# Weight sums and gate rows kept in DRAM in another layout, fetched in larger pieces, with VectorE's gating placed later in its order

## The chip, the core and the metric

The kernel runs on one core of one Trainium2 chip. The metric is the device time of one execution in microseconds (us). Each engine of the core (TensorE, here PE; VectorE, DVE; ScalarE, ACT; GpSimd, POOL; and the queue of SyncE, SP, which only issues transfers) works through its own list of instructions in program order and waits at semaphores for the others. PEld is TensorE's loading of weights.

## What is computed

One layer of a diffusion trunk on 1024 latent tokens (rows 0 to 7 of 128 tokens) and 128 context tokens (row 8). Both go through an input projection, a position-mixing group A and an attention group B; what concerns this change is the end of the attention and the output projection:

```python
def _back(x, gate, a_out, attn, g_b, w_o):
    y = jnp.concatenate([a_out, attn * jax.nn.silu(g_b)], axis=-1) @ w_o
    return x + gate * y
...
    y_sample = _rmsnorm(xs, final_g)
```

`gate` is a row of 1024 numbers for the latent tokens, another for the context tokens. `w_o` is 1024 x 1024.

## The kernel before

**Split operands.** Matmuls are done in three passes on a high and a low part of each operand (`hi`, `lo`), both stored as float32r. The high part is a rounded copy, the low part is what `lo_of` (L112, on VectorE) subtracts out.

**The output projection by Strassen-Winograd.** The product (latent rows) x `w_o` is done in 2 x 2 blocks with seven products for each pair of rows instead of eight. Four of the seven use a sum of blocks of `w_o` on the right: T1, T2, T3, T4. These *weight sums* depend on `w_o` alone. They are made during the attention in eight units (`t_unit`: subtractions on GpSimd, high part on ScalarE, low part on VectorE) and stored by SP in a DRAM tensor, `tdram` (L253): sum m, quarter k of the contraction, partition, part (high or low), 512 columns. Later they are fetched on GpSimd's DMA queue by `t_piece` (512 KB, both parts of one k) and `t_fetch` (256 KB, one part).

**Order during attention.** One head's scores are shifted by their maximum (`softmax`: L1481 and L1484 find the two maxima, then `nb` is made either by one instruction, L1489, or by a reduction and a product, L1486 and L1487), exponentiated on ScalarE (L1495) and scaled on GpSimd (L1501). Lists of spare work, `his` and `los`, are emptied a few jobs at a time after each head (`spare_hi`, `spare_lo`): splitting `w_o` (GpSimd, then VectorE), splitting row 8 and the first blocks, and the four sums of the first pair of rows (`s_sums`, L806 and L809 on GpSimd). T2 is fetched by a timed job, T3 by four jobs in `his`.

**The final stage.** `final` begins when the attention's tiles are given up (`c_at` is closed) and its tiles (`ep` pool) take their place. Here a small planner (`Plan`) sets the order: every step names its engine, a modelled cost and what it needs; a step is put out as soon as its engine is free and its needs are met in the model. Each engine then runs that order. Fetches are steps on a modelled engine D, one after the other: `gate0` (the latent gate row, read 128 times from `gdram`, 2 KB apart in four rows of 512), T1 and T4 in eight pieces on GpSimd's queue, `own1` (context gate and row 8 of x), rows of x, `fg`.

**Products and their banks.** The products of the final stage run in this order: three that were begun in the attention's last part (A11, A12 and S4 of pair 0, in PSUM banks f0, f1, f2), then S2, S3, S1 of pair 0 (trace names S2_0, S3_0, S1_0), A11 and A12 of pair 1, A22 of pair 0, and so on to pair 3. A product is 12 matmuls of 128 x 512 (L1923 to L1925). Its left operand lies in a ring of three slots (flat area, ringB, ringC), filled by ScalarE (L2149 copies the block to PSUM, L2151 makes the high part) and VectorE (L112, the low part; steps `lo3`, `lo4`, `lo5` for S2_0, S3_0, S1_0). The five PSUM banks are handed on: a product can start in a bank when the step that empties it is done. Bank f1 is emptied by step `m11` of pair 0 (L2197 on VectorE), which multiplies A12 by the gate row; S1_0 takes f1 next.

Of the kernel before, what the change touches and what calls it, by code (L numbers as in the profile page):

```python
# [18 lines left out]
P = 128  # L19
# [75 lines left out]
def tile_hymba_step(ctx: ExitStack, tc: tile.TileContext, I, O):  # L95
# [928 lines left out]
    def gate_steps(j):  # L1024
# [446 lines left out]
    def softmax(t, h, lat_, con_):  # L1471
# [11 lines left out]
        def shift():  # L1483
            V.tensor_reduce(m[:, 1:2], con_, axis=AX.X, op=ALU.max)  # L1484
            if units or his:
                V.tensor_reduce(nb, m, axis=AX.X, op=ALU.max)  # L1486
                V.tensor_scalar(nb, nb, nscl[:, t : t + 1], None, op0=ALU.mult)  # L1487
            else:
                V.scalar_tensor_tensor(nb, m[:, 0:1], m[:, 1:2], nscl[:, t : t + 1], op0=ALU.max, op1=ALU.mult)  # L1489
            later(0.6, exps)  # L1490
            later(1.3, lambda: spare_lo(1))
# [6 lines left out]
        def divide():  # L1498
# [3 lines left out]
            made.add(("e", t, h))  # L1502
            spare_hi(2)
            spare_lo(2)
# [107 lines left out]
    flat = []  # L1612
    for g in range(3):
        cols = area[g].rearrange("p a c -> p (a c)")
        flat.append([cols[:, n * 1024 : (n + 1) * 1024] for n in range(6)])


    his, los, rank = [], [], {}

# [168 lines left out]
    with tc.manual_schedule(engines=engines):  # L1788
# [52 lines left out]
        def first_jobs():  # L1841
# [31 lines left out]
        def t_unit(u, part, more):  # L1873
# [4 lines left out]
            def store(i, part_, src):  # L1878
                for m, j in ((1, 0), (3, 1), (4, 2), (2, 3))[2 * i : 2 * i + 2]:
                    nc.sync.dma_start(f32(tdram[m - 1, k][:, part_, 256 * c : 256 * c + 256]), src[:, j % 2, :])  # L1880

# [29 lines left out]

        def t_fetch(m, k, hi, lo):
            th[m, k], tl[m, k] = hi, lo
            for i, part in enumerate((hi, lo)):
                G.dma_start(part, tdram[m - 1, k][:, i, :])

        def t_piece(m, k, piece):
            th[m, k], tl[m, k] = piece[:, 0:512], piece[:, 512:1024]
            G.dma_start(piece, tdram[m - 1, k].rearrange("p s c -> p (s c)"))

# [105 lines left out]
    tpiece += [kv.tile([P, 1024], F32R, tag=n, name=f"{n}t") for n in ("vh", "vl")]  # L2026
    fg = ep.tile([P, 1024], F32, tag="fg", name="fg")
# [17 lines left out]

    def fetch(key, fn, deps=()):
        last_ = [fetched[0]] if fetched[0] else []
        step(key, "D", 1.35, fn, [*deps, *last_], 0, lag=1.8)
        fetched[0] = "|" + key

    def load_gate():
        gate[0] = ep.tile([P, 1024], F32, name="gate0", tag="gate0")
        nc.sync.dma_start(
            gate[0].rearrange("p (j r) -> p j r", j=4), gdram.rearrange("j (c r) -> c j r", c=2)[0:1].broadcast_to([P, 4, 256])
        )

    own = {}

    def load_own(i, dma):
        t_ = own[i] = ep.tile([P, 1024], F32, tag="xr", name=f"own{i}", bufs=4)  # L2060
        rows = gdram.rearrange("j (c r) -> c j r", c=2)[1:2, 2 * i : 2 * i + 2]
        dma(t_[:, 0:512].rearrange("p (j r) -> p j r", j=2), rows.broadcast_to([P, 2, 256]))
# [93 lines left out]
    for m in range(4):  # L2156
        plan.made[f"s{m}0"] = 0.0
        plan.made[f"T2{m}"] = plan.made[f"T3{m}"] = 0.0

# [17 lines left out]
    def pair(n):  # L2177
# [24 lines left out]
        if True:  # L2202
# [36 lines left out]
            for t in PAIRS[nx]:  # L2239
                fetch(f"x{t}", lambda t=t: load_xr(t), {2: [], 3: ["a81"]}.get(t, [f"y{t - 4}"]))  # L2240

    def products():
        for q in range(1, 28):
            n, name, m = queue[q]
            if q < 3:
                continue
            deps = [f"lo{q}", *([f"{m}{k}" for k in range(4)] if m[0] == "T" else [])]

# [166 lines left out]
```

## Time and profile before

| what | value |
|---|---|
| median of 3 runs | 626.22 us (624.83 to 626.61) |
| the profiled execution | 625.82 us |
| its span, first to last instruction | 624.0 us |
| time around the span | 1.82 us |
| VectorE, ScalarE, GpSimd busy | 428.7, 329.7, 207.8 us |
| bytes moved by DMA | 67.33 MB, mean 108 GB/s |

The profile lists, for one profiled execution, what each engine did at which time, what it waited for, and what the DMA queues moved. In the lists of instructions by time a row has the start in us, the length in us, engine, line, operation, output<-input, shapes and count, and in brackets the idle time of that engine just ahead of it with what ended it. In the tables by window a row has a stretch, its length, the busy time and number of instructions of PE, PEld, DVE, ACT and POOL, TensorE's granted clock as a share of full speed, the mean busy share of the 16 DMA engines, and GB/s. Queue q0 carries what GpSimd issues, q1 what SP issues, q10 what ScalarE issues; a queue's row has packets, MB and the share of the 16 engines' time.

### The profile page before, as it was taken

How to read it: one execution, taken by the hardware profiler on the slowest of the kernel's cores; microseconds unless marked ns; L12 is line 12 of the kernel's file. 1: busy time of each engine (PE TensorE's matmuls, PEld its weight loads, DVE VectorE, ACT ScalarE, POOL GpSimd, SP SyncE). 2: the span in 40 equal slices, each digit the busy share in tenths (PEclk: the TensorE clock that was granted, in tenths of full speed). 3: DMA queues.
4: the chain of work that ended last, by engine and by line, in shares of the span. 5: the costliest groups of instructions: out<-in, count | busy, mean ns of one | idle time of the engine just before them, and what ended most of it. 6: DMA issues, size and time to landing. Idle time of an engine off the chain costs nothing.

```text
span 624.0 us, 10238 instructions
## 1 busy us (share of the span) xinstructions
PE 599.9 (96%) x3671; PEld 540.1 (87%) x3671; DVE 428.7 (69%) x936; ACT 329.7 (53%) x765; POOL 207.8 (33%) x254
## 2 busy tenths in 40 slices
PE   7999999999999999999999999999999999599994
PEld 7578889999989999999988898998999888488884
DVE  3774458897755567566778677767778755268995
ACT  6556754336423345455676556665655543257543
POOL 2461111000000000333363354535434575059741
PEclk9999999999999999999999999999999999799998
DMA  8992010101262033000020143334410058850453
GB/s 309 367 392 86 1 34 2 35 1 46 100 232 84 14 119 125 20 1 1 2 74 1 35 136 126 125 126 133 135 69 35 1 185 241 282 170 8 161 154 151
DMA packets 32083, 67.33 MB, mean 108 GB/s; under 512 B 3472, under 2 KB 18592, under 8 KB 31520
## 3 DMA queue, kind: packets, MB, share of 16 engines
q1 hardware_dynamic: 27872, 55.41, 25.7%
q0 software_dynamic: 2880, 8.39, 4.2%
q10 hardware_dynamic: 1280, 2.88, 1.4%
q8 instruction: 29, 0.48, 0.3%
q14 instruction: 22, 0.18, 0.1%
HBM read 53.45 MB, written 13.21 MB: 107 GB/s over the span
## 4 chain that ended last, share of the span: by engine, by line
PE 76%; DVE 11%; DMA 5%; ACT 4%; issue 2%; SPq 0%; ACTq 0%; DVEq 0%
PE p L954 10%; PE tp L752 8%; PE tp L976 5%; DVE pl L112 4%; PE pT L1562 3%; DVE m L1481 2%; PE zacc L1390 2%; PE zacc L1391 2%; PE zacc L1389 2%; ACT e L1495 2%; PE S L1925 2%; PE S L1923 2%; PE S L1924 2%; DMA gate<-gdram 2%; DMA ada<-in_ada_ss 2%
## 5 line engine op out<-in xcount | busy, mean ns | idle before, releaser
L1501 POOL TENSOR_SCALAR e<-e,rs 128x1280 f32<-128x1280 f32 x32 | 47.0, 1467 | 100.6 <-ACT ph L1566 66.7
L112 DVE TENSOR_TENSOR pl<-pT,ph 128x512 fp32r<-128x512 f32 x81 | 55.4, 687 | 35.6 <-ACT ph L1566 33.8
L1495 ACT ACTIVATE e<-s,nb,scl 128x256 f32<-128x256 f32 x64 | 56.1, 880 | 43.3 <-DVE nb L1487 28.6
L1566 ACT CAST ph<-pT 128x512 fp32r<-128x512 f32 x80 | 46.3, 587 | 33.5 <-PE pT L1562 31.8
L1237 POOL TENSOR_TENSOR kr<-z,rope 128x64 f32<-128x64 f32 x8 | 2.6, 324 | 172.3 <-ACT z L1246 172.3
L752 PE MATMUL tp<-area,w 128*128 128x384 f32 x288 | 52.7, 339 | 0.0
L1562 PE MATMUL pT<-ident,e 128*128 128x128 f32 x320 | 48.4, 274 | 3.4 <-DVE pl L112 2.8
L752 PEld LDWEIGHTS tp<-area,w 128*128 128x128 f32 x288 | 50.6, 188 | 0.4
L1586 PE MATMUL o<-ph,vh 128*128 128x256 f32 x160 | 47.7, 298 | 0.0
L1588 PE MATMUL o<-ph,vl 128*128 128x256 f32 x160 | 45.0, 281 | 0.0
L1587 PE MATMUL o<-pl,vh 128*128 128x256 f32 x160 | 44.9, 281 | 0.0
L1562 PEld LDWEIGHTS pT<-ident,e 128*128 128x128 f32 x320 | 37.0, 140 | 8.4 <-PE at L1605 3.1
L1481 DVE TENSOR_REDUCE m<-s 128x1 f32<-128x1024 f32 x32 | 38.9, 1215 | 1.6 <-PE s L1519 1.6
L1515 PE MATMUL s<-kch,area 128*128 128x512 f32 (+2 forms) x100 | 39.1, 391 | 0.0
L1516 PE MATMUL s<-kcl,area 128*128 128x512 f32 (+2 forms) x100 | 35.3, 353 | 0.0
L1518 PE MATMUL s<-krh,area 128*128 128x512 f32 (+2 forms) x100 | 35.3, 353 | 0.0
L1517 PE MATMUL s<-kch,area 128*128 128x512 f32 (+2 forms) x100 | 35.1, 351 | 0.0
L1519 PE MATMUL s<-krl,area 128*128 128x512 f32 (+2 forms) x100 | 35.1, 351 | 0.0
L976 PE MATMUL tp<-area,w 128*128 128x384 f32 x192 | 35.0, 337 | 0.0
L976 PEld LDWEIGHTS tp<-area,w 128*128 128x128 f32 x192 | 33.6, 188 | 0.4 <-issue 0.4
L1587 PEld LDWEIGHTS o<-pl,vh 128*128 128x128 f32 x160 | 30.2, 189 | 1.3
L1586 PEld LDWEIGHTS o<-ph,vh 128*128 128x128 f32 x160 | 30.1, 188 | 1.4
(666 smaller groups left out, 1725.9 us busy)
## 6 DMA issues: line engine op xcount, KB each, us to landing
ada<-in_ada_ss SPq DMA_DIRECT2D x16, 512.0 KB, 8.5
w2r<-in_w_t SPq DMA_DIRECT2D x12, 512.0 KB, 4.3
x<-in_x SPq DMA_DIRECT2D x9, 512.0 KB, 7.6
adag<-in_ada_g SPq DMA_DIRECT2D x4, 1024.0 KB, 5.0
traw<-in_w_o SPq DMA_DIRECT2D x16, 256.0 KB, 3.5
tdram<-thi SPq DMA_DIRECT2D x32, 128.0 KB, 1.9
tdram<-traw SPq DMA_DIRECT2D x32, 128.0 KB, 1.8
wor<-in_w_o SPq DMA_DIRECT2D x8, 512.0 KB, 3.8
```

The lines of the kernel that those rows point to most:

```text
L112: V.tensor_tensor(lo, src, f32(hi), op=ALU.subtract)
L752: T.matmul(tps[i, g][:, :GW], w_[i][:, k, :], x_[k, g], start=k == 0 and j == 0, stop=k == NK - 1 and j == 2)
L954: T.matmul(banks[key], a_, b_, start=k == 0 and m == 0, stop=k == 3 and m == len(passes) - 1)
L976: T.matmul(tps[c, 2][:, :GW], w_[c][:, k, :], x_[k, 2], start=k == 0 and m == 0, stop=k == NK - 1 and m == 2)
L1481: V.tensor_reduce(m[:, 0:1], lat_, axis=AX.X, op=ALU.max)
L1495: S.activation(e[:, sl], src, AF.Exp, bias=nb, scale=scl[:, t : t + 1], accum_out=su[:, i : i + 1])
L1501: G.tensor_scalar(e, e, rs, 0.0, op0=ALU.mult, op1=ALU.add)
L1562: T.transpose(ps[:, w : w + P], es[t, h][:, c * P : (c + 1) * P], ident)
L1566: later(0.5, lambda: S.copy(ph[:, :w], ps[:, :w]))
L1586: T.matmul(o, vh[:, kt, :], ph[:, sl], start=c == 0, stop=False)
L1587: T.matmul(o, vh[:, kt, :], pl[:, sl], start=False, stop=False)
L1588: T.matmul(o, vl[:, kt, :], ph[:, sl], start=False, stop=c == n - 1)
```

## The change

The gate rows lie in DRAM as two rows of 1024 (latent, context), so that the fetch of `gate0` reads one run of 4 KB for each partition instead of four of 1 KB, and `own` one of 2 KB instead of two of 1 KB. `tdram` is laid out with a partition's four k side by side (16 KB from one partition to the next, 4 KB before), and `t_pieces` fetches two k in one issue of 1 MB: T2 and T1 by two issues each (8 KB runs for each partition), T3 by two (read in 8 KB runs, put in four runs of 2 KB), T4 by one of 1 MB and two of 512 KB. The one-instruction form of `nb` is used for every head without weight-sum units except the last. The list `heavy` holds the sums of pair 0, and one of them, not two, is done after a head while one is next. In the planner the gate counts as landed 4.5 us after its issue instead of 1.8, and T1 and T4 have costs by their sizes.

```diff
-    gdram = gd.tile([4, 512], F32, tag="gdram", name="gdram")
-    tdram = gd.tile([4, 4, P, 2, 512], F32R, tag="tdram", name="tdram")
+    gdram = gd.tile([2, 1024], F32, tag="gdram", name="gdram")
+    tdram = gd.tile([4, P, 4, 2, 512], F32R, tag="tdram", name="tdram")
...
-            nc.sync.dma_start(gdram[j : j + 1, :].rearrange("a (c r) -> (a c) r", c=2), cell["row"])
+            nc.sync.dma_start(gdram[:, 256 * j : 256 * j + 256], cell["row"])
...
-            if units or his:
+            if units or (t, h) == (NS - 1, 3):
...
-            spare_hi(2)
+            spare_hi(1 if his and his[0] in heavy else 2)
...
+                heavy.add(his[-1])
...
-        def t_fetch(m, k, hi, lo):
-            th[m, k], tl[m, k] = hi, lo
-            for i, part in enumerate((hi, lo)):
-                G.dma_start(part, tdram[m - 1, k][:, i, :])
-
-        def t_piece(m, k, piece):
-            th[m, k], tl[m, k] = piece[:, 0:512], piece[:, 512:1024]
-            G.dma_start(piece, tdram[m - 1, k].rearrange("p s c -> p (s c)"))
+        def t_pieces(m, k, hold, wide=512):
+
+            rows = hold.rearrange("p (a c) -> p a c", c=wide)[:, :, wide - 512 :]
+            n = rows.shape[1] // 2
+            for i in range(n):
+                th[m, k + i], tl[m, k + i] = rows[:, 2 * i], rows[:, 2 * i + 1]
+            G.dma_start(rows, tdram[m - 1, :, k : k + n].rearrange("p k s c -> p (k s) c"))
...
-                his.extend([lambda n=n: t_fetch(3, n, woh[n][:, 512:1024], wol[n][:, 512:1024]) for n in range(4)])
+                his.extend([lambda n=n: t_pieces(3, 2 * n, whole[n][:, 0:4096], 1024) for n in range(2)])
...
-        later(2.0, lambda: [t_piece(2, n, flat[2][2 + n]) for n in range(4)])
+        later(2.0, lambda: [t_pieces(2, 2 * n, whole[2][:, 2048 * n + 2048 : 2048 * n + 4096]) for n in range(2)])
...
-    tpiece = [ep.tile([P, 1024], F32R, tag=f"t{i}", name=f"tp{i}") for i in range(6)]
+    t1 = ep.tile([P, 4096], F32R, tag="t1", name="t1")
+    t4 = [ep.tile([P, 2048], F32R, tag="t4", name="t4"), *(kv.tile([P, 1024], F32R, tag=n, name=f"{n}t") for n in ("vh", "vl"))]
...
-    fetch("gate0", load_gate)
-    for m, n in ((1, 0), (4, 4)):
-        for k in range(4):
-            fetch(f"T{m}{k}", lambda m=m, k=k, n=n: t_piece(m, k, tpiece[n + k]))
+    fetch("gate0", load_gate, lag=4.5)
+    for k in (0, 2):
+        fetch(f"T1{k}", lambda k=k: t_pieces(1, k, t1[:, 1024 * k : 1024 * k + 2048]), cost=2.7)
+    for k, piece in ((0, t4[0]), (2, t4[1]), (3, t4[2])):
+        fetch(f"T4{k}", lambda k=k, piece=piece: t_pieces(4, k, piece), cost=1.35 if k else 2.7)
```

On VectorE, at the start of the final stage, before the change (mixB<-f1,gate0 is `m11`; the rows with raw3, raw4, raw5 are `lo3`, `lo4`, `lo5`):

```order
L806 TENSOR_TENSOR f1_5795<-f1_5795,mixA_95 128x512
L112 TENSOR_TENSOR area0_118<-raw3_6088,area0_118 128x512
L2197 TENSOR_TENSOR mixB_2045<-f1_5795,gate0_6074 128x4x128
L112 TENSOR_TENSOR ringB_5593<-raw4_6095,ringB_5593 128x512
L112 TENSOR_TENSOR ringC_5819<-raw5_6112,ringC_5819 128x512
L806 TENSOR_TENSOR mixA_95<-S2_0_6098,mixA_95 128x4x128
L112 TENSOR_TENSOR area0_118<-raw6_6133,area0_118 128x512
```

And with the change:

```order
L806 TENSOR_TENSOR f1_5790<-f1_5790,mixA_95 128x512
L112 TENSOR_TENSOR area0_118<-raw3_6072,area0_118 128x512
L112 TENSOR_TENSOR ringB_5590<-raw4_6078,ringB_5590 128x512
L112 TENSOR_TENSOR ringC_5828<-raw5_6094,ringC_5828 128x512
L2194 TENSOR_TENSOR mixB_2045<-f1_5790,gate0_6058 128x4x128
L806 TENSOR_TENSOR mixA_95<-S2_0_6080,mixA_95 128x4x128
L112 TENSOR_TENSOR area0_118<-raw6_6115,area0_118 128x512
```

`m11` stood ahead of `lo4` and `lo5` and stands behind them now; nothing else moved there. TensorE's order is the same. But S1_0 follows `m11` in bank f1, so its first matmul now waits for `m11`; before, `m11` was done whenever `lo4` was.

On GpSimd, from the scaling of head (7, 1) (e71) to the fetch of T1, before:

```order
L809 TENSOR_TENSOR mixB_2045<-mixA_95 128x4x128
L1501 TENSOR_SCALAR e72_5668<-e72_5668,rs72_5667 128x1280
L809 TENSOR_TENSOR mixA_95<-mixA_95 128x4x128
L809 TENSOR_TENSOR mixB_2045<-mixB_2045 128x4x128
L1501 TENSOR_SCALAR e73_5737<-e73_5737,rs73_5736 128x1280
L115 TENSOR_SCALAR ringC_5819<-mixB_2045 128x512
L1919 DMA area2_120<-tdram_92 128x1024
```

And with the change (area2<-tdram is the fetch of T2):

```order
L1501 TENSOR_SCALAR e72_5664<-e72_5664,rs72_5663 128x1280
L809 TENSOR_TENSOR mixB_2045<-mixA_95 128x4x128
L1501 TENSOR_SCALAR e73_5731<-e73_5731,rs73_5730 128x1280
L809 TENSOR_TENSOR mixA_95<-mixA_95 128x4x128
L809 TENSOR_TENSOR mixB_2045<-mixB_2045 128x4x128
L1919 DMA area2_120<-tdram_92 128x2048
L1919 DMA area2_120<-tdram_92 128x2048
L115 TENSOR_SCALAR ringC_5828<-mixB_2045 128x512
```

Each of the last three sums moved behind the scaling of the next head, and T2 is fetched ahead of the copy to ringC. Further on, all of T3 (three of eight pieces went ahead of it before) is fetched behind the split of the last quarter of `w_o` (wor7).

More of the change, by code (lines that the diff above doesn't have):

```diff
@@ L1612, in tile_hymba_step @@
     flat = []
-    for g in range(3):
-        cols = area[g].rearrange("p a c -> p (a c)")
+    whole = [area[g].rearrange("p a c -> p (a c)") for g in range(3)]
+    for cols in whole:
         flat.append([cols[:, n * 1024 : (n + 1) * 1024] for n in range(6)])
-    his, los, rank = [], [], {}
+    his, los, rank, heavy = [], [], {}, set()
     def split_job(hi, lo, key):
@@ L1879, in store @@
                 for m, j in ((1, 0), (3, 1), (4, 2), (2, 3))[2 * i : 2 * i + 2]:
-                    nc.sync.dma_start(f32(tdram[m - 1, k][:, part_, 256 * c : 256 * c + 256]), src[:, j % 2, :])
+                    nc.sync.dma_start(f32(tdram[m - 1, :, k, part_, 256 * c : 256 * c + 256]), src[:, j % 2, :])
             def high(i):
@@ L2044, in tile_hymba_step, with fetch @@
     fetched = [None]
-    def fetch(key, fn, deps=()):
+    def fetch(key, fn, deps=(), cost=1.35, lag=1.8):
         last_ = [fetched[0]] if fetched[0] else []
-        step(key, "D", 1.35, fn, [*deps, *last_], 0, lag=1.8)
+        step(key, "D", cost, fn, [*deps, *last_], 0, lag=lag)
         fetched[0] = "|" + key
@@ L2052, in load_gate @@
         gate[0] = ep.tile([P, 1024], F32, name="gate0", tag="gate0")
-        nc.sync.dma_start(
-            gate[0].rearrange("p (j r) -> p j r", j=4), gdram.rearrange("j (c r) -> c j r", c=2)[0:1].broadcast_to([P, 4, 256])
-        )
+        nc.sync.dma_start(gate[0], gdram[0:1, :].broadcast_to([P, 1024]))
     own = {}
@@ L2060, in load_own @@
         t_ = own[i] = ep.tile([P, 1024], F32, tag="xr", name=f"own{i}", bufs=4)
[L2061 to L2062 removed]
+        dma(t_[:, 0:512], gdram[1:2, 512 * i : 512 * i + 512].broadcast_to([P, 512]))
         dma(t_[:, 512:1024], I["x"][8][:, 512 * i : 512 * i + 512])
[L2065 to L2068 removed]
+    fetch("gate0", load_gate, lag=4.5)
[3 more added lines that the diff above has]
+        fetch(f"T4{k}", lambda k=k, piece=piece: t_pieces(4, k, piece), cost=1.35 if k else 2.7)
     fetch("own1", lambda: load_own(1, nc.scalar.dma_start))
@@ L2157, in tile_hymba_step @@
         plan.made[f"s{m}0"] = 0.0
-        plan.made[f"T2{m}"] = plan.made[f"T3{m}"] = 0.0
     turn = [None]
@@ L2240, in pair @@
                 fetch(f"x{t}", lambda t=t: load_xr(t), {2: [], 3: ["a81"]}.get(t, [f"y{t - 4}"]))
+    landed = dict(T1=("T10", "T12"), T4=("T40", "T42", "T43"))
     def products():
@@ L2246, in products @@
                 continue
-            deps = [f"lo{q}", *([f"{m}{k}" for k in range(4)] if m[0] == "T" else [])]
+            deps = [f"lo{q}", *landed.get(m, ())]
             def whole(q=q, n=n, name=name):
```

1 line of the change is left out of this document (removed).

## The prediction

> **What bounds the kernel now.** I read the busy table first, then the slices, the chain of waits, and last the rows by time where the chain leaves TensorE. The page's busy row of TensorE, its row of slices, and its row of the granted clock (40 slices of 15.6 us):
>
> ```profile
> PE 599.9 (96%) x3671; PEld 540.1 (87%) x3671; DVE 428.7 (69%) x936; ACT 329.7 (53%) x765; POOL 207.8 (33%) x254
> PE   7999999999999999999999999999999999599994
> PEclk9999999999999999999999999999999999799998
> ```
>
> TensorE is the bound: slices of 9 from the second to the last but one, with one hole, the 35th slice (530 to 546 us), where the clock falls too. The chain of waits names a transfer there, and the table by window shows the stage:
>
> ```profile
> 528.55 11.91 DMA gate<-gdram
> 541.90 0.80 PE S L1925
> 450.00:508.00 58.00, 56.68 (x393) 51.58 (x392) 44.42 (x94) 31.12 (x66) 28.89 (x29) 1.00 0.16 55
> 531.00:547.00 16.00, 9.02 (x31) 6.93 (x30) 3.76 (x7) 3.64 (x7) 1.29 (x1) 0.79 0.74 264
> 547.00:613.00 66.00, 66.00 (x302) 54.52 (x301) 55.27 (x92) 37.61 (x88) 42.38 (x32) 1.00 0.39 128
> ```
>
> From 547 to 613 TensorE never stops, so a product that starts earlier at 546 should carry the end with it. From 531 to 547 it works 9.02 of 16 us. VectorE's rows there, then TensorE's:
>
> ```profile
> 531.00 0.68 DVE L112 TENSOR_TENSOR area<-raw,area 128x512 fp32r<-128x512 f32 x1
> 540.55 0.69 DVE L2197 TENSOR_TENSOR mixB<-f,gate 128x512 f32<-128x512 f32 x1 [8.87 <-DMA gate<-gdram]
> 541.16 0.68 DVE L112 TENSOR_TENSOR ringB<-raw,ringB 128x512 fp32r<-128x512 f32 x1
> 531.58 0.39 PE L1923 MATMUL S<-area,area 128*128 128x512 f32 x1
> 534.30 0.39 PE L1923 MATMUL S<-area,ringB 128*128 128x512 f32 x1
> 534.53 0.39 PE L1924 MATMUL S<-area,ringB 128*128 128x512 f32 x1
> 541.90 0.80 PE L1925 MATMUL S<-area,ringB 128*128 128x512 f32 x1 [6.98 <-DVE ringB L112]
> 546.30 0.40 PE L1923 MATMUL S<-tp,ringC 128*128 128x512 f32 x1
> ```
>
> VectorE stands at `m11` until the gate row lands, and behind it stands `lo4`, for which S3_0's third matmul waits. The 512 KB gate fetch took 12.0 us, since T1 and T4, 4 MB, moved beside it.
>
> **Term 1: the hole.** One product takes 534.30 - 531.58 = 2.72 us. Unhindered, S3_0 would end and S1_0 begin at 534.30 + 2.72 = 537.02; it began at 546.30. The hole is 9.28 us: some 7.1 us of idling, and 2.1 us because the ten matmuls behind it took 4.40 us instead of 2.27. The clock explains that:
>
> ```profile
> 539.00:540.00 1.00, 0.00 (x0) 0.00 (x0) 0.00 (x0) 0.00 (x0) 0.00 (x0) 0.71 1.14 416
> 540.00:541.00 1.00, 0.00 (x0) 0.00 (x0) 0.45 (x1) 0.00 (x0) 0.00 (x0) 0.50 1.06 401
> 546.00:547.00 1.00, 1.00 (x5) 0.81 (x4) 0.00 (x0) 0.80 (x2) 0.00 (x0) 0.87 0.00 0
> ```
>
> In the new order `lo4` and `lo5` need only ScalarE's copies, which are there in time:
>
> ```profile
> 532.12 1.10 ACT L2149 COPY raw<-mixA 128x512 f32<-128x512 f32 x2
> ```
>
> Both end by 533.2, so VectorE ends `lo4` and `lo5` by about 534.6; S3_0's third matmul is due at 534.76. The hole goes at that place: **-9.28 us**.
>
> **Term 2: the last head's shift.** L1489 is long where GpSimd works beside it:
>
> ```profile
> 502.40 1.29 POOL L809 TENSOR_TENSOR mixB<-mixB 128x512 f32<-128x512 f32 x1
> 502.81 0.89 DVE L1489 SCALAR_TENSOR_TENSOR nb<-m,nscl 128x1 f32<-128x1 f32 x1
> 506.89 0.66 PE L1562 MATMUL pT<-ident,e 128*128 128x128 f32 x4 [0.72 <-DVE pl L112]
> L1486 DVE TENSOR_REDUCE nb<-m x20: 154/154/156, 348.9 to 496.9; 128x1 f32<-128x2 f32 x20
> L1487 DVE TENSOR_SCALAR nb<-nb,nscl x20: 212/214/216, 349.1 to 497.1; 128x1 f32<-128x1 f32 x20
> L1489 DVE SCALAR_TENSOR_TENSOR nb<-m,nscl x12: 219/254/1160, 318.1 to 502.8; 128x1 f32<-128x1 f32 x12
> ```
>
> It ended at 503.70 with GpSimd's subtraction (503.69). The two-step form takes 0.40 us here with its gap, so the exponentials, the transposes and TensorE, which idled 0.72 us for them, come **0.49 us** sooner; everything below moves with that. The other five heads go the other way, to L1489: 0.15 us less each where GpSimd is quiet, up to 0.8 us more where it is not (1160 against 370 ns), so +4 us at worst. I take 0: TensorE works 56.68 of 58 us in that stage, so little can be gained, and by the rows of before GpSimd's job ends before or at most 0.4 us behind those five places, as here (the shift comes at 484.39):
>
> ```profile
> 484.06 0.62 POOL L115 TENSOR_SCALAR area<-mixB 128x512 fp32r<-128x512 f32 x1
> ```
>
> **Term 3: the new wait.** S1_0 now waits for `m11`, so for the gate. How the gate shared the queues, in the stretches 532 to 533 and 534 to 535; then the issue of `own` and its queue, almost alone, from 550 to 551 and 551 to 552; last T3's and T1's queue from 526 to 527:
>
> ```profile
> q1 hardware_dynamic: 12, 0.01, 4.5%
> q0 software_dynamic: 78, 0.29, 78.3%
> q1 hardware_dynamic: 85, 0.09, 31.4%
> 549.14 0.40 ACTq L2062 DMA_DIRECT2D own<-gdram  x1
> q10 hardware_dynamic: 126, 0.13, 41.0%
> q10 hardware_dynamic: 144, 0.16, 103.6%
> q0 software_dynamic: 156, 0.29, 106.7%
> ```
>
> Its first packets moved some 4.2 us after the issue at 528.55, behind what q0 had in hand; then they went one to one with T's packets (85 beside 78), 512 of 1 KB in some 6.3 us; `m11` began 1.25 us after the last. Now there are 128 packets of 4 KB, each beside one of 8 KB: 128 x 12 KB = 1.57 MB at 0.38 MB/us is 4.1 us. So `m11` starts at 528.55 - 0.49 + 4.2 + 4.1 + 1.25 = 537.6 and S1_0 0.75 us later (541.16 to 541.90 above), at 538.36, where TensorE would be free at 537.02 - 0.49 = 536.53: **+1.83 us**. Bounds: a start of packets within 1.1 us of the issue, as `own` has it (issue 549.14, packets from 550.2), gives `m11` at 534.5 and no wait; a gate that is no sooner than before gives 540.06, S1_0 at 540.81, +4.28. An idle time of 4.3 us may also halve the clock (it fell 4.2 to 5.2 us into the hole), another 2.1. I take the middle, since its three parts each have a row.
>
> **What is hidden.** Fewer T issues save nothing: POOL's eight of T1 and T4 (0.53 us each) were ahead of the transfers. Behind `m11` on VectorE stand S2_0's addition and `lo6`, needed when S1_0 ends at 541.1; 537.6 + three of 0.68 is 539.6. The sums on GpSimd:
>
> ```profile
> 506.22 1.33 POOL L1501 TENSOR_SCALAR e<-e,rs 128x1280 f32<-128x1280 f32 x1 [2.54 <-ACT ph L1566]
> 507.52 0.62 POOL L115 TENSOR_SCALAR ringC<-mixB 128x512 fp32r<-128x512 f32 x1
> 520.51 1.34 POOL L115 TENSOR_SCALAR area<-wor 128x512 fp32r<-128x512 f32 x2 [6.10 <-DMA wor<-in_w_o]
> 525.86 3.18 POOL L1919 DMA_DIRECT2D tp<-tdram x6 [1.35 <-PE pT L1562]
> 512.62 0.69 DVE L112 TENSOR_TENSOR pl<-pT,ph 128x512 fp32r<-128x512 f32 x1 [2.07 <-ACT ph L1566]
> ```
>
> ringC's copy comes 2.6 us of sums and 1.1 us of T2's issues later, near 511.2; VectorE's subtraction for it holds up the `pl` of 512.62 by about 0.4 us, which TensorE reads near 515: 0, and 0.4 if that cover goes. T2, later by 2 us, is needed at 531. T3 goes whole behind wor7 (520.51): 2.1 MB in 2 KB runs at 0.29 MB/us (526 to 527) from 522.6 ends near 529.8, needed at 534.3. T1 then follows: its second MB, with gate and rows of x beside it, ends near 536.5 and lands near 537.7; S1_0 needs that half at 539.7. The 64 stores to `tdram` end 60 us ahead of the first fetch.
>
> **The sum.** -9.28 - 0.49 + 1.83 = -7.94. The profiled execution was 625.82 us (624.0 of span and 1.82 around it): 617.9 us. It lies 0.4 below the median of 626.22, so against that the gain may read as 8.3.
>
> **The rivals.**
> *The gate lands as late as before.* T's larger packets hog the engines. For it: q0 had 3 times q1's bytes in each us. Against: one to one by packets, the gate needs a quarter as many turns. By the bounds above 625.82 - 9.28 - 0.49 + 4.28 = 620.3, or 622.4 with the clock halved. The Trainium skill, "TensorE: Matmul & The Clock Gate" (The HAM clock gate), has the clock at half after about 3.4 us of idling; by that this case would be 622.4. Here the fall came 4.2 us or more into the hole, which is looser.
>
> *The weight sums come slower than before, and it ends slower.* A partition's row now lies 16 KB from the next instead of 4. T3, T1 and the gate, 4.7 MB, move from 522.6 on; the hole is as costly as before if the second half of T1 lands after some 545.5, so below 4.7 / (545.5 - 1.25 - 522.6) = 0.22 MB/us. `own` shows 0.16, the nearest slow row: then T1 lands at 553, 7 us behind, about 633. Against it: 8 KB runs of another tensor, 1 MB, landed in 5.0 us,
>
> ```profile
> adag<-in_ada_g SPq DMA_DIRECT2D x4, 1024.0 KB, 5.0
> ```
>
> and `own`'s runs are 1 KB. The Trainium skill, "DMA: Bandwidth & Descriptors" (Latency and other measured facts), tells of copies slowed to 207 GB/s by a row pitch of 512 KiB; carried to this pitch, which is an estimate far outside it, it would give about this case's threshold. No run here shows such a pitch yet.
>
> *The wait only moves.* `m11` at 544 or later, behind all T, with the clock halved: within 0.3%, about 625.
>
> **How the numbers follow.** Forecast (S1_0 between 536.5 and 540): 0.60, 617.9, from 616.0 to 619.5. Gate as late as before: 0.24, 620.3 to 622.4. Slower weight sums: 0.08, of which 0.06 end slower. The wait only moves or another hides the gain: 0.08, 0.05 of it within 0.3% (1.9 us, about what a measurement of this kernel can tell from no change). Range 615.5 to 622.4: from the case without a wait, less half a us, to the gate's worst bound. Faster 0.87, same 0.06, slower 0.07.
>
> **What would show it.** In the changed profile `lo4` and `lo5` should run before 535 and ahead of `m11`; S3_0 should have no gap at its third matmul; TensorE's next gap, if any, should stand at S1_0's first matmul with `m11` ahead of it and be 0 to 2.5 us; the clock should stay near 1.00 there; q1 should show 128 gate packets ending near 536.3. At the last head L1487 should end near 503.2. I am wrong if the gap at S1_0 is ended by a fetch of T1, or if TensorE waits anew between 450 and 531.

## The result, and the profile after

| | before | changed |
|---|---|---|
| median | 625.86 us (624.83 to 626.61, 4 runs) | 617.44 us (616.81 to 617.60, 4 runs) |
| the profiled execution | 625.82 us | 616.81 us |
| its span | 624.0 us | 615.0 us |

The ratio of the times is 0.9865, 95% interval 0.9848 to 0.9882: 8.4 us less by the medians, 9.0 us by the two profiled executions. The forecast was 617.9 us, 7.9 us less than the profiled execution.

The page of the changed kernel, its busy row of TensorE, the row of slices and the row of the granted clock:

```profile
PE 597.7 (97%) x3671; PEld 540.0 (88%) x3671; DVE 426.2 (69%) x932; ACT 330.0 (54%) x765; POOL 204.7 (33%) x243
PE   7999999999999999999999999999999999999994
PEclk9999999999999999999999999999999999999998
```

The 35th slice is a 9 like its neighbours, and the clock no longer dips there. The table by window of the changed kernel, for the stage of the heads and the start of the final stage:

```profile
450.00:508.00 58.00, 57.42 (x401) 52.54 (x400) 44.31 (x91) 31.34 (x66) 27.62 (x28) 1.00 0.15 53
531.00:547.00 16.00, 14.66 (x65) 11.77 (x64) 8.98 (x14) 6.14 (x12) 3.85 (x3) 1.00 0.93 342
```

From 531 to 547 TensorE works 14.66 of 16 us, where it worked 9.02, at a clock of 1.00 for 0.79. It also gained a little in the stage ahead, 57.42 of 58 us for 56.68. VectorE's rows of the changed kernel, `lo4`, `lo5` and `m11`:

```profile
531.60 0.69 DVE L112 TENSOR_TENSOR ringB<-raw,ringB 128x512 fp32r<-128x512 f32 x1 [1.03 <-ACT raw L2147]
532.21 0.68 DVE L112 TENSOR_TENSOR ringC<-raw,ringC 128x512 fp32r<-128x512 f32 x1
536.59 0.69 DVE L2194 TENSOR_TENSOR mixB<-f,gate 128x512 f32<-128x512 f32 x1 [3.70 <-DMA gate<-gdram]
```

VectorE still waits for the gate, 3.70 us for 8.87, but with `lo4` and `lo5` behind it. TensorE's rows: the first matmul of S2_0, the first and third of S3_0, the last of S3_0, and the first of S1_0:

```profile
530.45 0.39 PE L1923 MATMUL S<-area,area 128*128 128x512 f32 x1
533.17 0.39 PE L1923 MATMUL S<-area,ringB 128*128 128x512 f32 x1
533.62 0.39 PE L1925 MATMUL S<-area,ringB 128*128 128x512 f32 x1
535.66 0.39 PE L1925 MATMUL S<-area,ringB 128*128 128x512 f32 x1
537.38 0.47 PE L1923 MATMUL S<-t,ringC 128*128 128x512 f32 x1 [1.34 <-ACT raw L2147]
```

S3_0's third matmul follows its neighbours at once. The one gap left in this stage stands at S1_0, 1.34 us. The row blames a copy on ScalarE, but the matmul came 0.10 us after `m11` ended (536.59 + 0.69 = 537.28): a wait for several semaphores is put down to one of them, and here VectorE's row tells which it was.

How the gate's queue (q1) and T's (q0) shared the engines in the changed kernel, in the stretches 530.44 to 531.44 and 531.44 to 532.44, three and four us after the gate's issue at 527.44:

```profile
q0 software_dynamic: 50, 0.37, 93.8%
q1 hardware_dynamic: 11, 0.05, 12.0%
...
q0 software_dynamic: 31, 0.25, 69.6%
q1 hardware_dynamic: 31, 0.13, 33.6%
```

The first packet moved near 530.9, 3.4 us after the issue. Then the gate went one to one with T's packets, 31 of 4 KB beside 31 of 8 KB in the second stretch, and its 128 were through near 535.0.

**One measure for all kernels below.** Where a program has come to when the heads begin differs by up to 2.9 us between executions, also without the change: the shift `nb` that is at 447.84 in the kernel before stands at 449.14 in e1, which has nothing of the change up to there, and at 447.35 to 450.23 elsewhere. Much of this goes with the clock at the program's start. Where the granted clock over the first 30 us was 1.00 (the kernel before, e3, e9) the shift stands at 447.35 to 447.84; where it was 0.94 (changed, e2, e5), at 447.78 to 448.60; where it was 0.89 (the other eight), at 448.57 to 450.23. So I measure in each trace from that shift to the first matmul of A11_1, the product behind S1_0. Behind it every span goes on for 74.7 to 74.9 us, but for e6b with 75.4, so the gain lies between. And as the hole I take the time from S2_0's first matmul to A11_1's, less 8.24 us, which is the shortest seen (e11, without any gap). "Gate" is the time from the gate's issue to the start of `m11`.

| kernel | median us | ratio to before, interval | shift to A11_1, us | against before | hole | gate |
|---|---|---|---|---|---|---|
| before | 625.86 | | 101.25 | | 9.27 | 12.00 |
| changed | 617.44 | 0.9865, 0.9848 to 0.9882 | 92.48 | -8.77 | 1.57 | 9.15 |
| changed, once more (e12) | 617.75 | 0.9845, 0.9808 to 0.9882 | 92.14 | -9.11 | 1.29 | 8.90 |
| e1, order alone | 623.69 | 0.9955, 0.9928 to 0.9982 | 98.28 | -2.97 | 6.22 | 11.41 |
| e2, gate rows alone | 621.38 | 0.9910, 0.9878 to 0.9942 | 97.41 | -3.84 | 5.34 | 8.69 |
| e3, changed, old order | 621.66 | 0.9920, 0.9893 to 0.9947 | 97.55 | -3.70 | 6.27 | 8.39 |
| e4, changed, old weight sums | 616.73 | 0.9834, 0.9794 to 0.9874 | 92.15 | -9.10 | 0.41 | 8.03 |
| e5, changed, old heads | 617.28 | 0.9856, 0.9828 to 0.9883 | 92.89 | -8.36 | 0.86 | 8.47 |
| e6, five heads in two steps | 618.34 | 0.9873, 0.9850 to 0.9896 | 92.70 | -8.55 | 0.79 | 8.39 |
| e6b, last head in one step | 617.11 | 0.9854, 0.9828 to 0.9880 | 92.04 | -9.21 | 1.39 | 8.99 |
| e8, gate's tile first | 615.76 | 0.9828, 0.9800 to 0.9856 | 91.37 | -9.88 | 0.48 | at most 8.29 |
| e9, that and one step | 615.85 | 0.9822, 0.9788 to 0.9857 | 91.32 | -9.93 | 0.60 | 8.78 |
| e10, gate in 2 KB runs | 620.41 | 0.9894, 0.9861 to 0.9928 | 95.58 | -5.67 | 4.30 | 10.38 |
| e11, before, order, tile first | 618.00 | 0.9850, 0.9815 to 0.9886 | 92.06 | -9.19 | 0.00 | at most 8.29 |

The kernel before had medians of 626.44 beside e1 to e4, 626.30 beside e5, e6, e6b and e8, and 626.12 beside e9 to e12. Medians of kernels that ran at different times are compared by their ratios.

### The profile page after: what moved, and what is told of

Its sections match the earlier page's. It is cut to its first block, busy times and chain, and to the rows that moved or that the text cites. A ratio compares the mean times of both kernels' runs of the same rounds, so it can differ in the third digit from the quotient of the medians.

```text
span 615.0 us, 10220 instructions
## 1 busy us (share of the span) xinstructions
PE 597.7 (97%) x3671; PEld 540.0 (88%) x3671; DVE 426.2 (69%) x932; ACT 330.0 (54%) x765; POOL 204.7 (33%) x243
## 3 DMA queue, kind: packets, MB, share of 16 engines
q0 software_dynamic: 2064, 8.39, 4.0%
q10 hardware_dynamic: 1152, 2.88, 1.2%
## 4 chain that ended last, share of the span: by engine, by line
PE 81%; DVE 10%; ACT 4%; issue 2%; DMA 1%; SPq 0%; ACTq 0%; DVEq 0%
PE p L954 10%; PE tp L752 8%; PE tp L976 5%; PE pT L1562 4%; DVE pl L112 3%; PE zacc L1390 2%; PE zacc L1389 2%; PE zacc L1391 2%; PE S L1923 2%; DVE m L1481 2%; PE S L1924 2%; PE S L1925 2%; ACT e L1495 2%; PE s L1518 2%; PE s L1516 2%
## 5 line engine op out<-in xcount | busy, mean ns | idle before, releaser
L1562 PE MATMUL pT<-ident,e 128*128 128x128 f32 x320 | 48.4, 274 | 2.7 <-DVE pl L112 2.0
L1562 PEld LDWEIGHTS pT<-ident,e 128*128 128x128 f32 x320 | 37.0, 140 | 7.5 <-PE at L1605 2.5
```

The lines of the kernel that those rows point to most:

```text
L1562: T.transpose(ps[:, w : w + P], es[t, h][:, c * P : (c + 1) * P], ident)
```

## The experiments

My theory (A) was that the hole goes because VectorE does `lo4` and `lo5` ahead of `m11`, and that the gate's layout only shortens the wait that is left. The rivals: (B) larger pieces of the weight sums free the queues; (C) the gate's layout is the gain. The first four kernels take the change apart along these lines.

### e1: the order alone

```diff
-    def fetch(key, fn, deps=()):
+    def fetch(key, fn, deps=(), lag=1.8):
...
-        step(key, "D", 1.35, fn, [*deps, *last_], 0, lag=1.8)
+        step(key, "D", 1.35, fn, [*deps, *last_], 0, lag=lag)
...
-    fetch("gate0", load_gate)
+    fetch("gate0", load_gate, lag=4.5)
```

> The kernel before with nothing changed but the lag of the gate's fetch in the plan (1.8 to 4.5), so that VectorE has lo4 and lo5 ahead of m11; gate rows, weight sums and heads as before. Theory A (the gain is the order; the gate's layout only shortens the wait that is left): lo4 ends near 532 and S3_0 runs without a gap; the gate lands as late as before (m11 near 540.5), so TensorE waits some 4.3 us at S1_0's first matmul (537.0 to 541.3): 625.8 - 9.3 + 4.3 = 620.8, up to 622.9 if the clock halves. Rival B (what counts is that larger pieces of T free the queues): the order alone gains little, 624 to 626. Rival C (the gate's layout is the gain): the same, 624 to 626.

VectorE's and TensorE's rows of e1, `m11` and the first matmul of S1_0:

```profile
541.37 0.69 DVE L2197 TENSOR_TENSOR mixB<-f,gate 128x512 f32<-128x512 f32 x1 [5.96 <-DMA gate<-gdram]
542.16 0.76 PE L1923 MATMUL S<-tp,ringC 128*128 128x512 f32 x1 [3.60 <-issue]
```

The wait moved from S3_0's third matmul to S1_0's first, and shrank from 6.98 to 3.60 us, the `m11` behind it standing under the name "issue". The clock fell all the same, as e1's table by window shows:

```profile
540.00:541.00 1.00, 0.00 (x0) 0.00 (x0) 0.00 (x0) 0.00 (x0) 0.00 (x0) 0.90 1.14 411
541.00:542.00 1.00, 0.00 (x0) 0.00 (x0) 0.63 (x2) 0.00 (x0) 0.00 (x0) 0.50 1.09 414
```

The hole is 6.22 us: 3.60 of idling, and most of the rest is what half speed cost (S1_0's twelve matmuls took 5.26 us, for 2.88 in the changed kernel). The time, 623.69 us, lies between A's upper figure and what B and C gave. It is 2.75 us less than before (626.44), where A's figures, made from 625.8, meant 2.9 to 5.0: A is right about what happens, and the gain is just under its small end, the one with the clock halved.

### e2: the gate's rows alone

```diff
-    gdram = gd.tile([4, 512], F32, tag="gdram", name="gdram")
+    gdram = gd.tile([2, 1024], F32, tag="gdram", name="gdram")
...
-        nc.sync.dma_start(
-            gate[0].rearrange("p (j r) -> p j r", j=4), gdram.rearrange("j (c r) -> c j r", c=2)[0:1].broadcast_to([P, 4, 256])
-        )
+        nc.sync.dma_start(gate[0], gdram[0:1, :].broadcast_to([P, 1024]))
```

with the store and `own` as in the change.

> The kernel before with only the gate's rows in DRAM changed to two rows of 1024 (the store, the gate's fetch, own's fetch); order, weight sums and heads as before. Theory A: the gate's 128 packets of 4 KB go one to one with T's packets of 4 KB, some 3 us instead of 6.3, so m11 starts near 537, lo4 ends near 538.3 where S3_0's third matmul is due at 534.8: a hole of about 3.5 us in place of 9.3, 619.5 to 620.5, 622 if the clock halves. Rival B (T's pieces decide): the gate lands near 540 as before, 625 to 626. Rival C (the gate's layout alone is the gain): as good as the changed kernel, 617 to 618.

e2's row of TensorE at S3_0's third matmul, then two stretches of its table by window:

```profile
539.43 0.79 PE L1925 MATMUL S<-area,ringB 128*128 128x512 f32 x1 [3.66 <-DVE ringB L112]
```

```profile
538.00:539.00 1.00, 0.00 (x0) 0.00 (x0) 0.91 (x2) 0.00 (x0) 0.00 (x0) 0.99 1.07 401
539.00:540.00 1.00, 0.57 (x1) 0.50 (x2) 1.00 (x3) 0.59 (x1) 0.00 (x0) 0.50 1.11 410
```

The gate took 8.69 us for 12.00, the hole fell to 5.34, 3.66 of it idling. 621.38 us lies in A's span, 5.1 below before (3.84 by its trace): the layout alone saved more than the order alone. C, which wanted all of the gain from it, falls, and so does B; but A's "only shortens" was too small a word.

### e3: the changed kernel in the old order

```diff
-    fetch("gate0", load_gate, lag=4.5)
+    fetch("gate0", load_gate)
```

> The changed kernel with the lag of the gate's fetch back at 1.8, so that VectorE has m11 ahead of lo4 and lo5 again; gate rows, weight sums and heads as changed. Theory A: m11 starts at 536.6 as in the changed kernel, lo4 ends near 537.9 where S3_0's third matmul is due at 533.6: a gap of about 4.3 us there, and none at S1_0 (1.5): 616.8 + 4.3 - 1.5 = 619.6, up to 621.7 if the clock halves. Rival B (the layout and the larger pieces carry the gain): within 0.3 per cent of the changed kernel, 616 to 618. Rival C (the gate's layout): the same, 616 to 618.

e3's row at S3_0's third matmul, and the stretch of its table by window in which the clock fell:

```profile
537.25 0.80 PE L1925 MATMUL S<-area,ringB 128*128 128x512 f32 x1 [3.39 <-DVE ringB L112]
```

```profile
536.00:537.00 1.00, 0.00 (x0) 0.00 (x0) 1.00 (x2) 0.00 (x0) 0.00 (x0) 0.53 1.05 406
```

621.66 us, as A had it with the clock halved, and no better than e2, which has the old weight sums and heads. By the traces e3 is 5.1 to 5.4 us behind the changed kernel (97.55 against 92.48 and 92.14). About 0.4 us of that lies ahead of S2_0, where the order can't act: TensorE waited 0.32 us at 519.76 for `krl`, a low part of `w_o` that took VectorE 1.08 us for 0.68, beside GpSimd's split of wor7; e6 and e10 have the same wait. By the hole the order is worth 4.7 to 5.0 us here (6.27 against 1.57 and 1.29), and only 3.05 in e1 (9.27 against 6.22): the two together keep the wait so short that the clock stays.

### e4: the changed kernel with the old weight sums

`tdram`, `t_fetch`, `t_piece` and the eight fetches as before:

```diff
-    tdram = gd.tile([4, P, 4, 2, 512], F32R, tag="tdram", name="tdram")
+    tdram = gd.tile([4, 4, P, 2, 512], F32R, tag="tdram", name="tdram")
...
-        fetch(f"T1{k}", lambda k=k: t_pieces(1, k, t1[:, 1024 * k : 1024 * k + 2048]), cost=2.7)
+            fetch(f"T{m}{k}", lambda m=m, k=k, n=n: t_piece(m, k, tpiece[n + k]))
```

> The changed kernel with the weight sums' old layout in DRAM and their old 512 KB issues; the gate's rows, the order and the heads stay as changed. Theory A (merging T's issues adds nothing): T's packets beside the gate are 4 KB instead of 8, so the gate lands up to 1.4 us sooner or at the same time; 615.5 to 617.8. Rival B (larger pieces free the queues, so the gate lands early): the gate lands as late as before, near 540, and S1_0 waits 3 to 4 us more: 619.5 to 621. Rival C (the gate's layout): 617 to 618.

616.73 us: B falls. Beside T's packets of 4 KB the gate took 8.03 us, the shortest of all kernels that issue it at that place, and the hole was 0.41. The merged issues do save something elsewhere. In e4, GpSimd's four issues of T2 and the copy to ringC behind them, then TensorE's row:

```profile
509.64 2.34 POOL L1920 DMA_DIRECT2D area<-tdram  x4
511.98 0.66 POOL L115 TENSOR_SCALAR ringC<-mixB 128x512 fp32r<-128x512 f32 x1
```

```profile
514.16 0.66 PE L1562 MATMUL pT<-ident,e 128*128 128x128 f32 x4 [0.50 <-DVE mixB L1607]
```

Two issues take 1.28 us in the changed kernel, so ringC's copy comes 1.1 us sooner behind them, and there is no such gap. In e4 S2_0 starts 0.8 to 0.9 us later than in the changed kernel (83.50 us after the shift, for 82.67 and 82.61), 0.50 of it in this gap. The gate, in turn, had packets of T of half the size beside it: from 533.03 to 534.03 e4 moved 44 of the gate's beside 50 of T's, where the changed kernel moved 31 beside 31. So merging gives 0.8 to 0.9 us ahead of S2_0 and takes as much or a little more behind it (hole 1.57 and 1.29 for 0.41): no gain in sum.

### e5, e6, e6b: the heads

In the changed kernel S2_0 starts 82.67 us after the common shift, in the kernel before 83.74: 1.07 us came from the heads, where 0.49 was forecast. e5 has both lines of the heads as before; e6 only the two steps at the five heads; e6b one step at the last.

```diff
e5:
-            if units or (t, h) == (NS - 1, 3):
+            if units or his:
...
-            spare_hi(1 if his and his[0] in heavy else 2)
+            spare_hi(2)
e6:
-            if units or (t, h) == (NS - 1, 3):
+            if units or his or (t, h) == (NS - 1, 3):
e6b:
-            if units or (t, h) == (NS - 1, 3):
+            if units:
```

> The changed kernel with the attention heads' shift and GpSimd's spare jobs as before (two steps wherever a spare job is left, L1489 at the last head, two jobs a head); layouts and order as changed. Theory A (the heads are worth 1.1 us, what S2_0's start gained in the changed kernel against 0.49 forecast): S2_0 starts 1.1 us later, 617.9 to 618.5. Rival D (that 1.1 us is scatter between executions, and only the forecast 0.49 is real): S2_0 starts 0.4 to 0.6 us later, 617.3 to 617.9. Rival E (heads are worth nothing): within 0.2 us of the changed kernel.

S2_0 started 83.79 us after the shift, 1.12 later than in the changed kernel, as A had it. But the time is 617.28 us, which can't be told from the changed kernel: of the 1.12 us, 0.71 came back at S1_0 (hole 0.86 for 1.57). What ties the two is argued from the traces, not shown by a run of its own: T3's issue stands behind GpSimd's split of wor7 and did not come sooner with the heads. It stood 9.2 us ahead of the gate's in e5 and 7.4 in the changed kernel, so that more of T was ahead of the gate. In the kernels with the changed rows and weight sums the gate took 8.4 to 8.5 us where T3 stood 8.4 us or more ahead (e3, e5, e6), and 8.9 to 9.2 where it stood 7.4 ahead (changed, e6b, e12). Five us after its issue the gate moved beside shorter packets in e5: 41 in a us beside 39 of T's that held 0.20 MB, for 31 beside 28 with 0.20 MB in the changed kernel.

> The changed kernel with the two-step shift at the five heads that still have spare jobs behind them, as before, and at the last head as changed; GpSimd's jobs spread as changed. Theory A (the five shorter shifts brought some 0.6 us, where the forecast had 0): S2_0 starts 0.5 to 0.7 us later than in the changed kernel, 617.3 to 618. Rival D (those five are hidden, as forecast): S2_0 within 0.2 us of the changed kernel, 616.7 to 617.3.

The last head's shift came 54.99 us after the common one, for 54.37 in the changed kernel and 54.97 before: the five heads give 0.62 us, as A had it. A further 0.38 us was lost ahead of S2_0 (TensorE waited 0.31 us for `krl` at 521.84, as in e3 and e10, which have the heads as changed, so that part is not the heads'). The median, 618.34, is above A's span.

> The changed kernel with the one-step shift L1489 at the last head too; GpSimd's jobs spread as changed, so one subtraction now stands behind the last head's scaling of e instead of two ahead of it. Theory A (the two-step form is what shortened the last head): L1489 is held by GpSimd's job as before, near 0.9 us, and S2_0 starts 0.4 to 0.5 us later, 617.2 to 617.8. Rival F (moving GpSimd's jobs alone freed that place): L1489 takes 0.22 us there, and the time is that of the changed kernel or 0.2 us less.

Here I was wrong and rival F right. The shift of the last head, in e5 beside GpSimd's subtraction, then in e6b:

```profile
502.76 0.91 DVE L1489 SCALAR_TENSOR_TENSOR nb<-m,nscl 128x1 f32<-128x1 f32 x1
```

```profile
502.37 1.29 POOL L809 TENSOR_TENSOR mixB<-mixB 128x512 f32<-128x512 f32 x1
```

```profile
503.53 0.22 DVE L1489 SCALAR_TENSOR_TENSOR nb<-m,nscl 128x1 f32<-128x1 f32 x1
```

With `spare_hi(1)` GpSimd has no job there: in the changed kernel its last subtraction ahead of that place ends at 501.79, and the shift stands at 502.15. One step takes 0.22 us there and 0.40 in two, and e6b is 0.26 us quicker to S2_0 (82.41 us). The gain at the last head came from GpSimd's moved job; the two-step form took a part of it back.

### e8: the gate's tile first

```diff
+    gate = {0: ep.tile([P, 1024], F32, name="gate0", tag="gate0")}
     t1 = ep.tile([P, 4096], F32R, tag="t1", name="t1")
...
-        gate[0] = ep.tile([P, 1024], F32, name="gate0", tag="gate0")
```

> The changed kernel with the gate's tile taken from its pool ahead of T1's, so that it lies where room comes free sooner. Theory A (what is left of the wait at S1_0 is the gate's landing, which hangs on its issue): the issue moves from 527.4 towards 525.2, m11 starts near 534.5 to 535, S1_0 begins behind S3_0 without a gap, 1.3 to 1.5 us less than the changed kernel: 615.3 to 616. Rival B (the gate's packets wait for T3's, already in the queues, whenever it is issued): m11 stays near 536.5, and the time is that of the changed kernel, 616.7 to 617.6. Against both: if T1 or T4, whose tiles lie 4 KB further, is issued later for it, TensorE waits for T1 at S1_0 and it is slower than the changed kernel.

e8's gate issue on SP's queue, `m11` on VectorE, and on TensorE the first matmuls of S1_0 and of its second half:

```profile
525.42 0.33 SPq L2053 DMA_DIRECT2D gate<-gdram  x1
```

```profile
533.71 0.68 DVE L2194 TENSOR_TENSOR mixB<-f,gate 128x512 f32<-128x512 f32 x1
```

```profile
536.79 0.40 PE L1923 MATMUL S<-t,ringC 128*128 128x512 f32 x1
538.56 0.50 PE L1923 MATMUL S<-t,ringC 128*128 128x512 f32 x1 [0.20 <-DMA t<-tdram]
```

`m11` no longer waits for the gate and S1_0 begins with no gap; S2_0 begins at 531.35 here, so the issue is 2.9 us sooner measured from there (5.93 us ahead of S2_0, for 3.01). What is left is 0.20 us for the second half of T1. 615.76 us is what A expected.

### e9 to e12: the two together, the packets, the place, and the changed kernel again

e9 is e8 with e6b's line.

> The changed kernel with the gate's tile taken from its pool ahead of T1's, and the one-step shift at the last head too. Theory A (the two act in places of their own, and what the profiles of each alone showed adds up: 1.5 us at S1_0, 0.26 us at the last head): 1.4 to 1.8 us less than the changed kernel run beside it, S1_0 behind S3_0 with a gap of at most 0.4 us. Rival B (the second half of T1 or another landing now ends the wait, 0.2 us with the gate first): all that comes earlier on TensorE is waited for there, and the time is that of the gate first alone, 1.0 to 1.3 us less than the changed kernel.

615.85 us, 1.9 below the changed kernel beside it, but the intervals overlap. By the trace it is 0.82 us from the shift to A11_1 (91.32 against 92.14 in e12), and against e8 nothing: TensorE waits 0.34 us for T1 where e8 had 0.20. Rival B is nearer: T1 is the next bound.

e10 keeps a gate row as two runs of 512:

```diff
-    gdram = gd.tile([2, 1024], F32, tag="gdram", name="gdram")
+    gdram = gd.tile([2, 2, 512], F32, tag="gdram", name="gdram")
...
-        nc.sync.dma_start(gate[0], gdram[0:1, :].broadcast_to([P, 1024]))
+        nc.sync.dma_start(gate[0].rearrange("p (a r) -> p a r", a=2), gdram.rearrange("a c r -> c a r")[0:1].broadcast_to([P, 2, 512]))
```

with the store and `own` to match.

> The changed kernel with a gate row kept as two runs of 512 (2 KB) in DRAM, so 256 packets for the gate instead of 128; issue, order, weight sums and heads as changed. Theory A (the gate takes turns with T's packets one to one, so its time goes by the number of its packets): between the 8.0 to 9.2 us from issue to m11 with 128 packets and the 11.4 to 12.0 with 512, near 9.5 to 10.5; S1_0 waits 2.5 to 3.5 us instead of 1.5, and the time is 1 to 2 us above the changed kernel, more if the clock halves. Rival G (it goes by bytes, or only runs of 1 KB are slow): m11 8.0 to 9.2 us behind the issue, the time of the changed kernel. Rival H (one to one with 8 KB packets of T, 256 turns take as long as 512 turns beside 4 KB packets): 11.4 to 12 us, and S1_0 waits some 4 us.

The queues of e10 from 532.92 to 533.92, its row of S1_0, and the stretch after it:

```profile
q0 software_dynamic: 40, 0.33, 81.8%
q1 hardware_dynamic: 40, 0.08, 26.1%
```

```profile
540.09 0.47 PE L1923 MATMUL S<-t,ringC 128*128 128x512 f32 x1 [2.53 <-issue]
```

```profile
541.00:542.00 1.00, 1.00 (x4) 0.81 (x3) 0.78 (x2) 0.00 (x0) 0.00 (x0) 0.50 1.05 381
```

Forty to forty: packet by packet, whatever their sizes. 256 packets took 10.38 us, in A's span, and the time is 2.7 us above e12, since 2.53 us of idling cost half the clock for another 3.4 us.

e11 is e1 with the gate's tile first, as in e8: rows, weight sums and heads are those of the kernel before.

> The kernel before with the lag of the gate's fetch at 4.5 (lo4 and lo5 ahead of m11) and the gate's tile taken from its pool ahead of T1's, as with the gate first; gate rows, weight sums and heads as before. Theory A (only when the gate lands counts, by an earlier issue as well as by fewer packets): the issue comes 2.1 us sooner than with the order alone, m11 11.4 to 12 us behind it, so TensorE waits some 1.5 to 2.2 us at S1_0 instead of 3.8 and the clock stays: 618.5 to 619.5 beside 626.3 of before. Rival C (without the gate's layout the fetch of 1 KB runs is slow enough to hold TensorE as long): 621 to 624.

e11's gate issue, its `m11`, and the gate's queue from 528.83 to 529.83:

```profile
526.83 0.38 SPq L2053 DMA_DIRECT2D gate<-gdram  x1
```

```profile
535.12 0.68 DVE L2197 TENSOR_TENSOR mixB<-f,gate 128x512 f32<-128x512 f32 x1
```

```profile
q1 hardware_dynamic: 180, 0.18, 85.4%
```

No wait at S1_0 at all, and 618.00 us beside 617.75 for the changed kernel: the order and an earlier place of one tile did as much as the whole change. It beat A's figure too. Between T3's last packets and T1's first (the first six issues of T1 and T4 run from 527.48 to 530.66) the gate had q0 out of its way: 180 packets in that us, where 85 moved beside T in the kernel before. The 512 packets cost what is in the queue beside them, and A had carried over the 11.4 to 12 us of the crowded place.

e12:

> The changed kernel once more, on the same chip as the other three. All theories: 617.0 to 617.8, ratio 0.984 to 0.988.

617.75 us, ratio 0.9845: as expected.

## Why the prediction was right, step by step

**The hole.** "The hole goes at that place: -9.28" held: S3_0's third matmul has no gap, and `lo4` and `lo5` ended at 532.29 and 532.89, ahead of the forecast 534.6. The order alone only moves the wait to S1_0 (e1), the case of the upper bound in term 3; it nearly goes where the gate also lands sooner, by its rows (the changed kernel) or by its tile's place (e11). What the prediction gave no price for is the gate's rows by themselves: order and rows alone are worth 2.97 and 3.84 us by the traces, together with the rest 8.77 to 9.11.

**The new wait.** It came where it was put, with the parts that the prediction had: first packets 3.4 us after the issue (4.2 forecast), 128 packets one to one with T's in 4.1 us (4.1), `m11` 1.6 us behind the last (1.25). S1_0 came 1.49 us after TensorE was free (537.38 against 533.17 + 2.72 = 535.89), forecast 1.83. e10 shows that the turns go by packets, which the term rested on, and e1 shows the case of the upper bound: "622.4 with the clock halved" was the gate as late as before in the new order, and e1's profiled execution took 624.06 us, with the common shift 1.3 us late already.

**The last head's shift** was the term whose size was off: forecast 0.49 us, measured 1.07 by S2_0's start. Two reasons. The five other heads, which "I take 0", gave 0.6 us. These are two of them in the changed kernel, the second beside a sum on GpSimd:

```profile
477.70 0.22 DVE L1489 SCALAR_TENSOR_TENSOR nb<-m,nscl 128x1 f32<-128x1 f32 x1
...
496.25 0.40 DVE L1489 SCALAR_TENSOR_TENSOR nb<-m,nscl 128x1 f32<-128x1 f32 x1
```

None came near the feared 1160 ns, and the 0.15 us a head was not hidden. I had argued from TensorE's 56.68 busy us of 58 that little was to be gained; but of the 1.3 us of gaps 0.72 stood behind the last head's shift, and the rest behind two of these five, in rows of the kernel before that I had not looked for:

```profile
485.54 0.63 PE L1562 MATMUL pT<-ident,e 128*128 128x128 f32 x4 [0.26 <-DVE pl L112]
498.06 0.63 PE L1562 MATMUL pT<-ident,e 128*128 128x128 f32 x4 [0.32 <-DVE pl L112]
```

They stand 1.15 us behind the shifts of 484.39 and 496.91 and make 0.58 us together; the changed kernel has nothing of the first and 0.17 us of the second, so 0.41 of the 0.6 us. The other 0.2 us shows behind the first of the five, though the list has no gap there: from the start of `at` (L1605) to that of the next transposes (L1562) TensorE took 0.63 us in the kernel before (460.39 to 461.02) and 0.46 in the changed one (460.33 to 460.79). And the last head's 0.49 us was right by luck: the changed kernel gained about 0.45 there (1.07 less the five heads' 0.62), but for another reason: the two-step form was priced beside a job on GpSimd that the same change moves away. The section on the change had listed that move.

**The sum.** By the traces the gain is 8.77 us: 9.27 of the hole, less 1.57 that is left, and 1.07 ahead of S2_0. The forecast of 7.94 was too small by 0.26 at the new wait and by 0.58 at the heads. The rest of the 9.0 us between the two profiled executions lies outside: 0.06 ahead of the common shift and 0.17 behind A11_1.

**What is hidden.** That fewer T issues save nothing was right in the sum (e4), not in each place. ringC's copy, "0.4 if that cover goes", lost its cover in e4: 0.50 us.

**The rivals.** The gate did not land as late as before. The weight sums did not slow down at a pitch of 16 KB: from 529.44 to 530.44, when T1 and T4 alone move in the changed kernel, q0 made 0.41 MB/us, where the threshold was 0.22 and the kernel before, at its pitch of 4 KB, had 0.39 from 532 to 533 (the 0.29 of 526 to 527 was in packets of 1.9 KB):

```profile
q0 software_dynamic: 60, 0.41, 108.3%
```

The Trainium skill, "DMA: Bandwidth & Descriptors" (Latency and other measured facts), has 207 GB/s at a pitch of 512 KiB beside 214 at full rate, a loss of 3%, and 164 at 2 MiB; I took the first for a slow one, and nothing follows from it for this pitch. At 16 KB this trace shows nothing slow. The clock stayed at 1.00 in the gap of 1.34 us.

## What to carry to other kernels

An engine that does its work in order should not stand at a transfer while ready work that TensorE needs soon lies behind it; but look also at when the transfer is issued and what is in the queues at that time, since one tile taken earlier from its pool did as much here as a new layout. A small transfer behind a long one is paid by its number of packets, so make them few or send it into a quiet moment. And price a moved instruction beside what will run there after the change, not beside what ran there before.

## What the hardware showed that I had not expected

**The clock falls and rises in steps of 3.4 us that don't follow the wait.** By the quarter us in the tables by window:

| kernel | TensorE idle | clock fell | after it stopped | half speed for |
|---|---|---|---|---|
| before | 534.92 to 541.90 | 539.43 | 4.5 us | 6.8 us |
| e1 | 538.56 to 542.16 | 540.81 | 2.3 us | 6.8 us |
| e2 | 535.77 to 539.43 | 539.00 | 3.2 us | 3.4 us |
| e3 | 533.86 to 537.25 | 536.05 | 2.2 us | 6.8 us |
| e10 | 537.56 to 540.09 | 540.88 | 3.3 us, 0.8 after it went on | 3.4 us |
| changed | 536.05 to 537.38 | not | | |

The prediction had read the one fall that it could see as a delay of 4.2 to 5.2 us. The Trainium skill, "TensorE: Matmul & The Clock Gate" (What's actually happening), has a window of 3413 ns that runs freely, and the durations of half speed, once and twice 3.4 us, agree with it. The stretch ahead of a fall need not be wholly idle: the 3.41 us ahead of e1's fall had 1.17 us of matmuls in them, up to 538.56, and e10's wait of 2.53 us was enough. Nor does the clock rise with the first matmul. In the first 3.41 us of half speed TensorE was busy for 0.94 us in the kernel before, 2.06 in e1 and 2.22 in e3, and a second 3.4 us followed; with 2.97 us in e2 and 3.41 in e10 the clock rose. So two waits of nearly the same length cost two steps in e1 (3.60 us) and one in e2 (3.66). This would fit the scatter of e3, from 618.99 to 623.48 us in its 11 runs, with a mean granted clock of 0.997 in the quickest and 0.985 to 0.987 in the four longest. But the program's start has such steps too (1.00 to 0.89 over the first 30 us), and no clock of those executions by the us is at hand to tell the two apart. The gaps of 1.06 and 1.34 us in the changed kernel's two profiles, and of 0.63 in e5, left the clock at 1.00.

**A queue that starts late shares by packets.** After its issue the gate moved nothing for 3.4 us in the changed kernel, and then as many packets as T's queue, where T's were of 8 KB and the gate's of 4 (31 to 31) and where they were of 8 and 2 (40 to 40). What holds it up in those 3.4 us stays open; in e8 the first packets came 2 us and more after the issue and in e11 about 1 us, with T3's still in q0.

Not tried: the gate's tile first in the old order, which by e8's `m11` (ended 534.39, where `lo4` would end near 535) would by my estimate leave a gap of at most about half a us at S3_0's third matmul, and a T1 issued sooner for e9.
